# A hybrid RWKV-7 / mLSTM layer with a mixture of experts: the estimate behind TensorE's order is refitted, GpSimd's tensor work moves to VectorE and ScalarE, and the chain's PSUM tiles go into two banks

## The chip, the cores and the metric

The kernel runs on one core of one Trainium2 chip. The metric is device time in microseconds for one launch, the median of three runs. A matrix product is issued to TensorE (PE), elementwise work to VectorE (DVE), ScalarE (ACT) and GpSimd (POOL), transfers mostly from SyncE's queue (SP). In the code these engines are P, V, S, G and Y.

## The reference, cut to what matters

528 tokens (512 and 16 meta tokens) of width 1024 go through one hybrid layer and a mixture of experts, all in float32.

```
xn   = rmsnorm(h);  proj = xn @ w_in                # r, k, v | q, k, v, o, gates
# RWKV-7, 8 heads of 64, a state S of 64 x 64 per head, token by token
Sa = S @ a_t
S  = S * d_t + outer(Sa, b_t) + outer(v_t, k_t);   y_t = S @ r_t
# (low-rank products give the decay d and the gates a, g; y is normalised and gated)
# mLSTM, 4 heads, in chunks of 64 tokens, normalised and gated by sigmoid(o)
h  = h + concat(y_a, y_b) @ w_out
xn = rmsnorm(h)
# router: top-1 of 4 groups, top-2 of 8 experts in it
y[tok] += gate * ((silu(gt) * up) @ w_dn[e]),  gt, up = split(x[tok] @ w_gu[e])
```

## The kernel before, in words

**Stages.** The RWKV recurrence is turned into chunks of 64 tokens. At the start (to about 30 us) x is split into a high and a low part (`xh`, `xl`), the first two blocks of w_in are multiplied as three products of such parts, and `squares` (L613) sums x squared into the tile `acc`; two pairs of matmuls with a matrix of ones then give the norm. Up to 165 us the other blocks of w_in follow (`PLAN`, L34: one letter a block of 128 columns, each weight split into a high part by ScalarE and a low part by `lo_by` in `prepare`, L671), with four pairs of RWKV heads prepared between them (`heads`, L836, and `products`, L902). From 160 to 224 us the triangular matrices of all chunks are inverted: small blocks by VectorE elementwise (`interleaved`, L1335), the 16 meta tokens' own block by GpSimd (`inverse0`, L1357), then 32x32 matmuls (`inverse`, L1372). The chain (`chain`, L1476) runs over a chunk of 16 tokens and eight of 64, in order: `removals` and `solved` give each chunk's corrected values, `next_state` the state, `outputs` the chunk's y. To 300 us it is interleaved with what is left of the projections, of the mLSTM heads and of the states. Then come norms and gates (`outputs_a`, L1567, `gated`, L1576), the product with w_out, the router, and from 435 us the experts: 16 passes of two experts, each with 12 MB of weights.

**The order of the work.** Every instruction goes through one recording helper (line L304 of the profile). TensorE has one queue, in order. The generators of all those stages are woven into it by `Weave` (L355): by rank, and by an estimate, `Clock` (L181), of when each operand is ready. `cost` (L239) gives an instruction's duration, `slot` (L226) its place on an engine, `tell` (L273) writes end times into 16-column by 32-partition cells of each tile. A generator whose next operand the estimate puts later than now waits (`need`), and another one's matmuls are put ahead. The estimate decides the order when the program is built; on the chip each instruction waits for semaphores.

**PSUM.** `accs` has eight banks. Banks 0 to 3 are `lead`, 4 to 7 `rest`; of these 4 and 5 are `small`, 6 and 7 `wide` (L500). In the chain, `pU` takes 4 and 5 and `pY` takes 6 and 7. Each of the four banks holds one or two tiles of 256 columns: `pW` (removals) and the first half of `uv` (solved) are in 4, `pS` (next state) and the other half of `uv` in 5, the two halves of `yv` (outputs) in 6 and 7. The halves, p = 0 and p = 1, are partitions 0 to 63 and 64 to 127. ScalarE copies the first half of `uv` out and both halves of `yv`, VectorE the other half of `uv`, and VectorE adds `pS` to the decayed state `SD`, in two instructions.

```
for ch in range(-1, 8):
    removals(ch, first, vs, n);  yield from need(Wt)
    solved(ch, first, vu, n);    yield from need(vu)
    next_state(ch, first, vu, nxt)
    outputs(ch, vs, vu)
```

Of the kernel before, what the change touches and what calls it, by code (L numbers as in the profile page):

```python
# [17 lines left out]
L = 528  # L18
# [162 lines left out]
class Clock:  # L181
# [3 lines left out]
    EACH = {"V": (0.08, 1.05e-3), "S": (0.07, 0.88e-3), "G": (0.16, 0.85e-3)}  # L185
    LAG = 0.139

    def __init__(self):
        self.t = 0.0
        self.ticks = {}  # L190
        self.busy = {e: [] for e in "VSGY"}
        self.cells = {}
        self.table = None

    def cover(self, tile):

        n = int(np.prod(tile.shape[1:]))
        self.cells[tile.tensor.name] = np.zeros((2, 4, n // 16 + 1)), n

# [4 lines left out]
    def part(self, ap):  # L204
# [3 lines left out]
        c, n = self.cells[name]  # L208
# [17 lines left out]
    def slot(self, engine, ready, dur):  # L226
# [4 lines left out]
        for i, (a, b) in enumerate(busy):  # L231
            if a - ready >= dur:
                busy.insert(i, (ready, ready + dur))
                return ready
            ready = max(ready, b)
        busy.append((ready, ready + dur))
        return ready

    def cost(self, engine, op, outs, ins, kw):  # L239
# [18 lines left out]
        a, b = self.EACH[engine]  # L258
        if engine == "G" and op == "tensor_tensor":
            b = 2.1e-3  # L260
# [12 lines left out]
    def tell(self, engine, op, args, kw):  # L273
# [6 lines left out]
        ready = max(self.wrote(*ins), self.read(*outs) if engine == "P" else self.free(*outs)) + self.LAG  # L280
        if engine == "P":
            self.t = end = max(self.t, ready) + dur
        else:
            if "dma" in op:
                engine = "Y"
            end = self.slot(engine, ready, dur) + dur + (2.0 if engine == "Y" else 0)
        for ap in outs + ins:
            c = self.part(ap)
            if c is not None:
                k = 0 if any(ap is o for o in outs) else 1  # L290
                c[k] = np.maximum(c[k], end + (0.1 if engine == "P" and not k else 0))
# [19 lines left out]
class Banks:  # L311


    def __init__(self, t, clock):
        self.t, self.clock = t, clock
        clock.cover(t)
        self.busy = [False] * 8
# [118 lines left out]
def layer(ctx, tc, a, out, dbg=None, stop=None):  # L436
# [145 lines left out]
    acc = A.get([128, L], name="acc")  # L582
# [29 lines left out]
    A.put(idle_)  # L612
    def squares(k):  # L613
        sq = A.get([128, L], name="sq") if k else acc
        if k % 2:
            V.tensor_tensor(sq, xT[:, k], xT[:, k], op=OP.mult)
        else:
            S.activation(sq, xT[:, k], AF.Square)
        if k:
            G.tensor_tensor(acc, acc, sq, op=OP.add)  # L620
            A.put(sq)

    first_block(0, 2)
    for k in range(8):
# [10 lines left out]
        if k >= 2:  # L635
            proj_k(pk1, k1h, k1l, k)
            squares(k - 2)
    for k in range(6, 8):
        squares(k)

# [27 lines left out]
    def late():  # L668
        return len(every) == 8

    def prepare(kind):  # L671

        lo_by = V if late() and kind != "q" or "P3" not in W.marks else G
# [19 lines left out]
    pss = B.get(2, "pss", rest)  # L693
    for h in range(2):
        P.matmul(pss[:, h, :264], m("ones"), acc[:, 264 * h:264 * h + 264], start=True, stop=True)
# [4 lines left out]
    A.put(xT, acc)  # L700
# [135 lines left out]
    def heads():  # L836

        for j in range(4):
# [28 lines left out]
            G.tensor_scalar(r[:, NM:], r[:, NM:], c("r_k", j), 0.0, op0=OP.mult, op1=OP.add)  # L867
            G.tensor_tensor(r[:, NM:], r[:, NM:], kp[:, NM:], op=OP.mult)
# [322 lines left out]
    def states():  # L1191
# [3 lines left out]
        for tb in range(-1, 3):  # L1195
# [6 lines left out]
            kw = A.get([128, 4, 64], name="kw")  # L1202
# [154 lines left out]
    def inverse0():  # L1357
# [8 lines left out]
        yield from interleaved(G, XL0, lambda s: NL0[:, s + 1:, s], NM, tm0, 99)  # L1366
# [5 lines left out]
    def inverse():  # L1372
# [39 lines left out]
        A.put(NL, XL, Y1, Y2, *tmps, *Zs)  # L1412
        dump("X", Bt)
# [916 lines left out]
```

## Time and profile before

| what | value |
|---|---|
| median of 3 runs | 911.82 us (910.79 to 916.01) |
| profiled execution | 910.37 us |
| its span | 908.5 us |
| PE busy, share of the span | 843.5 us, 93% |
| DVE busy | 434.4 us, 48% |
| ACT busy | 270.9 us, 30% |
| POOL busy | 226.4 us, 25% |
| bytes moved by DMA | 235.56 MB, mean 259 GB/s |

The profiled execution lies 1.45 us under the median. The span runs from the first to the last record; the remaining 1.9 us are around it. Busy times of the engines overlap; the shares are means over stages that differ, and PE's 93% is made of stages in which it computes all the time and others in which it waits. A matmul of float32 is several passes, and a row's mean for one matmul is longer than what each adds to a row of many, since they are pipelined.

### The profile page before, as it was taken

The numbers are of one execution on the slowest core, as the hardware profiler recorded it, in microseconds if no ns is written. First come the engines' busy times: TensorE is split into PE (matmuls) and PEld (weight loads), VectorE is DVE, ScalarE is ACT, GpSimd is POOL, SyncE is SP. The second block draws the span as 40 slices with busy tenths as digits, with TensorE's granted clock in tenths as the row PEclk, the third lists the DMA queues.
The fourth block names the chain that finished last, engine by engine and source line by source line (L and its number), as shares of the span: only waits on it lengthen the run. The fifth ranks groups of instructions, "written<-read, shape, count | busy, mean of one in ns | idle before, by whom it ended". The sixth has DMA issues, their size and how long they took to land.

```text
span 908.5 us, 13524 instructions
## 1 busy us (share of the span) xinstructions
PE 843.5 (93%) x5385; PEld 522.1 (57%) x5386; DVE 434.4 (48%) x822; ACT 270.9 (30%) x522; POOL 226.4 (25%) x297
## 2 busy tenths in 40 slices
PE   7989889879999997998899999999999999989994
PEld 5878778769999776887334444334444333323331
DVE  7676766995544668327213334233334133322324
ACT  5666555434435773333101110011101011001102
POOL 6064544464545156254100000000000000000002
PEclk8989999987999999998899999999999999999998
DMA  7201123111100137929899999999999999999982
GB/s 237 71 3 46 47 69 83 47 47 53 51 25 25 48 107 291 403 71 335 335 402 419 420 420 420 421 420 420 420 419 421 420 421 420 420 421 421 420 341 96
DMA packets 45141, 235.56 MB, mean 259 GB/s; under 512 B 9906, under 2 KB 10290, under 8 KB 21008
## 3 DMA queue, kind: packets, MB, share of 16 engines
q1 hardware_dynamic: 42192, 228.56, 63.3%
q0 software_dynamic: 2160, 3.93, 1.2%
q10 hardware_dynamic: 720, 2.15, 0.6%
q8 instruction: 44, 0.72, 0.3%
q14 instruction: 25, 0.20, 0.1%
HBM read 234.36 MB, written 4.19 MB: 263 GB/s over the span
## 4 chain that ended last, share of the span: by engine, by line
PE 53%; DMA 24%; DVE 13%; ACT 4%; issue 2%; POOL 2%; SPq 0%; ACTq 0%; DVEq 0%; POOLq 0%
PE accs L304 25%; PE accs L2070 14%; DVE arF L304 8%; DMA arF<-wgu 7%; PE accs L2115 6%; DMA arF<-wdn 5%; DMA arM<-wgu 4%; ACT arF L304 3%; PE accs L1993 2%; DMA arH<-wgu 2%; DMA arN<-wgu 2%; DMA arN<-wdn 2%; PE accs L1994 2%; DMA arF<-wo 1%; POOL arF L304 1%
## 5 line engine op out<-in xcount | busy, mean ns | idle before, releaser
L304 PE MATMUL accs<-arS,arR 128*128 128x264 f32 (+2 forms) x1136 | 184.5, 314 | 10.2 <-DVE arR L304 5.0
L304 PEld LDWEIGHTS accs<-arS,arR 128*128 128x128 f32 (+1 forms) x1136 | 162.4, 200 | 22.5 <-DVE arR L304 5.5
L304 PE MATMUL accs<-arF 64*64 64x64 f32 (+18 forms) x1223 | 127.7, 268 | 27.5 <-DVE arF L304 17.4
L1996 DVE TENSOR_TENSOR arF<-arF,accs 128x512 f32<-128x512 f32 x124 | 80.7, 681 | 98.1 <-PE accs L1994 96.6
L304 PEld LDWEIGHTS accs<-arF 128*128 128x128 f32 (+7 forms) x1202 | 102.2, 157 | 37.3 <-DVE arF L304 11.4
L2070 PE MATMUL accs<-arF 128*64 128x512 f32 x488 | 116.4, 608 | 4.2 <-DMA arF<-wgu 4.2
L304 POOL TENSOR_TENSOR arF<-arF 128x528 f32<-128x528 f32 (+13 forms) x101 | 92.3, 917 | 67.6 <-DVE arF L304 45.4
L1804 POOL DMA_INDIRECT arM<-hd,arF x15 | 15.2, 1012 | 376.2 <-DVE arF L1794 362.7
L304 DVE TENSOR_TENSOR arF<-arF 64x16 f32<-64x16 f32 (+33 forms) x183 | 89.5, 535 | 5.1 <-POOL arF L304 2.8
L2092 ACT ACTIVATE arF<-accs,arF 128x512 f32<-128x512 f32 x16 | 11.0, 687 | 247.5 <-PE accs L2070 247.5
L2070 PEld LDWEIGHTS accs<-arF 128*64 128x64 f32 x488 | 32.6, 138 | 74.2 <-issue 57.5
L304 ACT ACTIVATE arF<-arF 128x528 f32<-128x528 f32 (+8 forms) x108 | 57.9, 559 | 49.8 <-DVE arF L304 35.5
L2125 DVE SCALAR_TENSOR_TENSOR arO<-accs,arF,arO 128x1024 fp32r<-128x1024 f32 x15 | 19.3, 1283 | 103.6 <-ACT arO L2124 103.6
L304 POOL TENSOR_SCALAR arF<-arF 64x256 f32<-64x256 f32 (+9 forms) x97 | 55.3, 572 | 42.6 <-ACT arF L304 19.6
L2115 PE MATMUL accs<-arF 128*64 128x512 f32 x280 | 62.3, 595 | 0.5 <-issue 0.5
L304 ACT COPY arF<-accs 64x256 f32<-64x256 f32 (+6 forms) x119 | 43.2, 370 | 64.1 <-PE accs L304 30.5
L1993 PE MATMUL accs<-arO,OHT 128*128 128x512 f32 x124 | 57.4, 463 | 0.0
L304 DVE TENSOR_TENSOR arF<-accs,arF 128x528 f32<-128x528 f32 (+7 forms) x81 | 35.4, 460 | 34.1 <-PE accs L304 20.6
L1994 PE MATMUL accs<-arO,OHT 128*128 128x512 f32 x124 | 48.9, 394 | 0.0
L2070 PE MATMUL accs<-arN,arF 128*64 128x512 f32 x200 | 47.1, 599 | 1.6 <-DMA arN<-wgu 1.6
L304 PE MATMUL accs<-arW,arS 128*128 128x512 f32 x192 | 47.8, 406 | 0.0
L2070 PE MATMUL accs<-arM,arF 128*64 128x512 f32 x200 | 46.7, 599 | 1.0 <-DMA arM<-wgu 0.9
(141 smaller groups left out, 932.6 us busy)
## 6 DMA issues: line engine op xcount, KB each, us to landing
arF<-wgu SPq DMA_DIRECT2D x61, 1024.0 KB, 19.8
arF<-wdn SPq DMA_DIRECT2D x35, 1024.0 KB, 20.1
arN<-wgu SPq DMA_DIRECT2D x25, 1024.0 KB, 19.9
arM<-wgu SPq DMA_DIRECT2D x25, 1024.0 KB, 19.8
arH<-wgu SPq DMA_DIRECT2D x16, 1024.0 KB, 19.9
arN<-wdn SPq DMA_DIRECT2D x15, 1024.0 KB, 19.9
arF<-wb SPq DMA_DIRECT2D x23, 512.0 KB, 3.6
arH<-wdn SPq DMA_DIRECT2D x5, 1024.0 KB, 19.8
```

Source lines behind the costliest of these rows:

```text
L304: r = f(*args, **kw)
L1804: nc.gpsimd.indirect_dma_start(out=xt[p % 2], out_offset=None, in_=hd, in_offset=bass.IndirectOffsetOnAxis(ap=idx[:, p % 2:p % 2 + 1], axi ...
L1993: P.matmul(pq, lhs, oh[:, hs], start=True, stop=False)
L1994: P.matmul(pq, lhs, ol[:, hs], start=False, stop=True)
L1996: V.tensor_tensor(hv, hv, pq, op=OP.add)
L2070: P.matmul(pgu[64 * e:64 * e + 64, h], x[:, k, 64 * e:64 * e + 64], w[:, D * e + 512 * h:D * e + 512 * h + 512], start=(k == 0), stop=(k = ...
L2092: S.activation(av, pgu[:, 0], AF.Silu, scale=r1_)
L2115: P.matmul(pdn[64 * e:64 * e + 64, h], aT[:, k, 64 * e:64 * e + 64], w[:, D * h + 512 * e:D * h + 512 * e + 512], start=(k == 0), stop=(k ...
L2125: V.scalar_tensor_tensor(ol, pdf, g1_, oh.bitcast(F32), op0=OP.mult, op1=OP.subtract)
```

## The change

In the estimate: new constants for ScalarE, GpSimd, matmuls by shape and the scan; a shorter delay (`NEAR`, 0.07) between instructions of one engine; an engine `X` that stands for the port which GpSimd and a VectorE instruction with two wide inputs in SBUF share, so that the estimate puts them one after the other. In the work: the squares go to ScalarE and their pairwise sums to VectorE, with four pairs of ones-matmuls in place of one pair, and no sum on GpSimd; three tensor products a head and the product with r_k go from GpSimd to VectorE; two copies into E a head go from GpSimd to ScalarE; `inverse0` and the gate of `gated` go to VectorE; the low parts of weights that are made between the products of the last pair of heads and the end of the inverse go from GpSimd to VectorE. In the chain: `uv` and `pW` lie in one bank, `pS` and `yv` in the other, and the two banks of `pY` are free for others. Some tiles of the end are taken in other places (`Gw`, `kw`, `sq`, `yT`).

```diff
-    EACH = {"V": (0.08, 1.05e-3), "S": (0.07, 0.88e-3), "G": (0.16, 0.85e-3)}
-    LAG = 0.139
+    EACH = {"V": (0.08, 1.05e-3), "S": (0.13, 0.88e-3), "G": (0.17, 0.9e-3)}
+    LAG, NEAR = 0.139, 0.07
...
-            m = size(ins[0])
-            n, passes = size(ins[1]), 2 if op == "transpose" else 4
+            m, n = size(ins[0]), size(ins[1])
             if ins[1].dtype == F32R and n >= 256 or ins[1].dtype == BF16:
-                passes = 1
-            dur = max(n, m) * passes / 2400 * (0.7 if m <= 64 and passes > 1 else 1.0)
+                passes, dur = 1, max(n * 1.09 / 2400, 0.056)
+            elif op == "transpose":
+                passes, dur = 1, 0.11
+            else:
+                passes, dur = 4, 2 * max(n * 2.05 / 2400, 0.055 if m <= 64 else 0.11)
...
+            if engine == "G" or engine == "V" and len(wide_) > 1:
+                engine += "X"
             end = self.slot(engine, ready, dur) + dur + (2.0 if engine == "Y" else 0)
...
     def squares(k):
-        sq = A.get([128, L], name="sq") if k else acc
+        sqs2.append(A.get([128, L], name="sq"))
+        S.activation(sqs2[k], xT[:, k], AF.Square)
         if k % 2:
-            V.tensor_tensor(sq, xT[:, k], xT[:, k], op=OP.mult)
-        else:
-            S.activation(sq, xT[:, k], AF.Square)
-        if k:
-            G.tensor_tensor(acc, acc, sq, op=OP.add)
-            A.put(sq)
+            V.tensor_tensor(sqs2[k], sqs2[k], sqs2[k - 1], op=OP.add)
...
-        lo_by = V if late() and kind != "q" or "P3" not in W.marks else G
+        lo_by = V if late() and kind != "q" or "inverse" not in W.marks else G
...
-            G.tensor_tensor(MV[:, :, 128:192], i64[:, None].to_broadcast([128, 8, 64]),
+            V.tensor_tensor(MV[:, :, 128:192], i64[:, None].to_broadcast([128, 8, 64]),
...
-            G.tensor_tensor(nk, nk, al, op=OP.mult)
+            V.tensor_tensor(nk, nk, al, op=OP.mult)
...
-            G.tensor_tensor(kp, kp, kx[j], op=OP.mult)
+            V.tensor_tensor(kp, kp, kx[j], op=OP.mult)
...
-                    (S.copy if p else gcopy)(E[i][PAR[p], :, j, p], MV[PAR[p], 4 * i:4 * i + 4, 0:128])
+                    S.copy(E[i][PAR[p], :, j, p], MV[PAR[p], 4 * i:4 * i + 4, 0:128])
...
-        yield from interleaved(G, XL0, lambda s: NL0[:, s + 1:, s], NM, tm0, 99)
+        yield from interleaved(V, XL0, lambda s: NL0[:, s + 1:, s], NM, tm0, 99)
...
-                P.matmul(uv[o, p, j], (X0[PAR[p], j] if first else Bt[PAR[p], ch, j, 0:64]), Wt[PAR[p], j],
+                P.matmul(uv[o, j], (X0[PAR[p], j] if first else Bt[PAR[p], ch, j, 0:64]), Wt[PAR[p], j],
...
-        pY = yield from bank(2, "pY", wide)
-        pW, pS = (pU[:, i, 256:512].rearrange("p (j x) -> p j x", j=4) for i in range(2))
-        uv = pU[:, :, 0:256].rearrange("p a (j x) -> p a j x", j=4)
-        yv = pY[:, :, 0:256].rearrange("p a (j x) -> p a j x", j=4)
+        (uv, pW), (pS, yv) = ([pU[:, i, 256 * h:256 * h + 256].rearrange("p (j x) -> p j x", j=4) for h in range(2)]
+                              for i in range(2))
...
-        G.tensor_tensor(y, y, Gw[:, :, 128 * tb:128 * tb + 128], op=OP.mult)
+        V.tensor_tensor(y, y, Gw[:, :, 128 * tb:128 * tb + 128], op=OP.mult)
```

What this moves shows in the instruction order at three places. The first is TensorE's queue in one chunk of the chain, with the semaphores that an instruction waits for in brackets. Before, eight matmuls of `next_state` (the first two rows) are followed by the sixteen of `outputs` (`arE` is the tile E), then by two matmuls of a projection:

```order
596 L304 MATMUL accs<-arF 64x64 [waits DVE_49,Activation_49]
597 L304 MATMUL accs<-arF 64x64 x7
598 L304 MATMUL accs<-arE_255,arF 64x64 x8
599 L304 MATMUL accs<-arF 64x64 x8
600 L304 MATMUL accs<-arS_68,arR 128x264 x2
```

With the change the same matmuls stand in the same order, followed by the next chunk's `removals`:

```order
623 L336 MATMUL accs<-arF 64x64 x4
624 L336 MATMUL accs<-arF 64x64 [waits DVE_49]
625 L336 MATMUL accs<-arF 64x64 x3
626 L336 MATMUL accs<-arE_258,arF 64x64 [waits DVE_49]
627 L336 MATMUL accs<-arE_258,arF 64x64 x7
628 L336 MATMUL accs<-arF 64x64 x4
629 L336 MATMUL accs<-arF 64x64 [waits Activation_49]
630 L336 MATMUL accs<-arF 64x64 x3
631 L336 MATMUL accs<-arF,arE_258 64x64 x8
```

The wait for ScalarE ahead of `next_state` is gone from this place, and two waits are new: `outputs` waits for VectorE before its first matmul, and for ScalarE before the second half's own four.

The second is the same queue at `solved`, a few rows earlier. Before, its eight matmuls stand behind one wait, between projections:

```order
587 L304 MATMUL accs<-arS_68,arR 128x264 [waits Pool_49]
588 L304 MATMUL accs<-arS_68,arR 128x264
589 L304 MATMUL accs<-arF 64x64 [waits DVE_49]
590 L304 MATMUL accs<-arF 64x64 x7
591 L304 MATMUL accs<-arS_68,arR 128x264 x2
```

and with the change:

```order
608 L336 MATMUL accs<-arS_68,arR 128x264 x2
609 L336 MATMUL accs<-arF 64x64 [waits DVE_49]
610 L336 MATMUL accs<-arF 64x64 x3
611 L336 MATMUL accs<-arF 64x64 [waits Activation_49]
612 L336 MATMUL accs<-arF 64x64 x3
613 L336 MATMUL accs<-arS_68,arR 128x264 x2
```

The second half now waits for ScalarE, which copies the first half out of the bank.

The third is GpSimd's queue while VectorE inverts. Before, the small steps of `inverse0` alternate with the low parts of weights (128x1024):

```order
92 L304 TENSOR_TENSOR arR<-arF,arR 128x1024
93 L304 TENSOR_TENSOR arF<-arF 128x63
94 L304 TENSOR_TENSOR arF<-arF 128x7x9
95 L304 TENSOR_TENSOR arF<-arF 128x64
96 L304 TENSOR_TENSOR arF<-arF 128x8x8
97 L304 TENSOR_TENSOR arF<-arF 128x63
```

With the change the queue holds at that place:

```order
49 L336 TENSOR_TENSOR arF<-arF 128x512 x2
50 L336 TENSOR_SCALAR arF<-arF 64x4x64 x2
51 L336 TENSOR_SCALAR arF<-arF 128x64
52 L336 MEMSET arF 128x3 x2
53 L336 TENSOR_SCALAR arF<-arF 64x4x64 x2
54 L336 MEMSET arF 128x256
55 L336 TENSOR_TENSOR arF<-arF 128x528
```

Those steps and the low parts have left GpSimd; they stand in VectorE's queue.

## Rows read from the trace of the kernel before

**Rows 1.** Busy times by stretch: us, engines (instructions), PEclk, DMA share, GB/s

```profile
195.00:298.00 103.00, 103.00 (x1311) 95.69 (x1310) 56.21 (x120) 45.16 (x87) 52.89 (x74) 0.89 0.11 34
410.00:435.00 25.00, 18.94 (x187) 17.31 (x186) 20.40 (x80) 7.62 (x26) 9.72 (x13) 0.81 0.91 340
...
656.00:860.00 204.00, 196.65 (x970) 73.80 (x966) 63.50 (x114) 20.82 (x28) 5.95 (x6) 1.00 1.01 420
```

**Rows 2.** The chain that ended last, around 655 us: start, us, what

```profile
654.60 1.44 PE accs L2070 x7
656.04 20.48 DMA arM<-wgu
```

**Rows 3.** Waits of PE, 0 to 435 us: in total, times, longest

```profile
PE accs L304 <- DVE arF L304: 18.4, 10, 6.0
PE accs L304 <- ACT arF L304: 8.1, 12, 2.0
...
PE accs L304 <- DVE arS L304: 3.1, 3, 2.0
```

**Rows 4.** Timeline of the start (PE, then DVE, then POOL): start, us, instructions, idle before

```profile
10.52 5.68 PE L304 MATMUL accs<-arS,arR 128*128 128x264 f32 x25 [2.00 <-DVE arS L304]
25.72 1.05 PE L304 MATMUL accs<-arF 128*128 128x264 f32 x4
27.93 0.75 PE L304 MATMUL accs<-arS,arQ 128*128 128x264 f32 x4 [1.16 <-ACT arQ L304]
17.44 0.79 DVE L304 SCALAR_TENSOR_TENSOR arS<-arF,arS 128x528 fp32r<-128x528 f32 x1
19.90 4.44 DVE L304 SCALAR_TENSOR_TENSOR arS<-arF,arS 128x528 fp32r<-128x528 f32 x3
17.76 6.02 POOL L304 TENSOR_TENSOR arF<-arF 128x528 f32<-128x528 f32 x4
```

**Rows 5.** Timeline, first pair of heads: DVE, POOL, PE

```profile
60.90 3.64 DVE L304 TENSOR_TENSOR arF<-arF 64x512 f32<-64x512 f32 x1 [2.84 <-POOL arF L304]
62.69 2.99 POOL L304 TENSOR_TENSOR arF<-arF 128x528 f32<-128x528 f32 x2
66.66 3.83 PE L304 MATMUL accs<-arF 128*128 128x192 f32 x12 [3.29 <-POOL arF L304]
```

**Rows 6.** Timeline of the elementwise inverse: DVE, POOL twice, PE

```profile
173.88 17.66 DVE L304 TENSOR_TENSOR arF<-arF 128x96 f32<-128x96 f32 x44
179.13 2.48 POOL L304 TENSOR_TENSOR arR<-arF,arR 128x1024 fp32r<-128x1024 f32 x1 [0.21 <-ACT arR L304]
181.57 4.62 POOL L304 TENSOR_TENSOR arF<-arF 128x63 f32<-128x63 f32 x10
194.25 2.62 PE L304 MATMUL accs<-arF 128*128 128x128 f32 x10 [6.00 <-DVE arF L304]
```

**Rows 7.** Timeline, norms and gates: DVE, PE

```profile
349.34 1.21 DVE L304 TENSOR_TENSOR arR<-arF,arR 128x1024 fp32r<-128x1024 f32 x1
350.61 5.64 PE L304 MATMUL accs<-arS,arR 128*128 128x512 f32 x17 [5.03 <-DVE arR L304]
```

**Rows 8.** Busy times of three shorter stretches, columns as in rows 1

```profile
9.00:15.80 6.80, 5.28 (x24) 5.28 (x25) 6.80 (x6) 5.85 (x10) 5.12 (x4) 0.50 1.05 382
193.30:200.10 6.80, 5.86 (x25) 5.22 (x26) 6.73 (x21) 1.87 (x6) 5.27 (x10) 0.50 0.01 2
213.80:227.40 13.60, 13.60 (x222) 13.29 (x221) 5.98 (x8) 5.14 (x10) 2.64 (x5) 0.50 0.20 66
```

**Rows 9.** Timeline of one chunk of the chain: PE, then DVE, then ACT

```profile
260.32 0.64 PE L304 MATMUL accs<-arE,arF 128*64 128x64 f32 x13
260.89 0.96 PE L304 MATMUL accs<-arF 64*64 64x64 f32 x16
261.78 0.69 PE L304 MATMUL accs<-arF,arE 128*64 128x64 f32 x16
260.60 0.88 DVE L304 TENSOR_TENSOR arF<-accs,arF 64x256 f32<-64x256 f32 x2 [2.19 <-PE accs L304]
261.60 0.75 ACT L304 COPY arF<-accs 64x256 f32<-64x256 f32 x2 [0.66 <-PE accs L304]
```

More of the change, by code (lines that the diff above doesn't have):

```diff
@@ L190, in __init__ @@
         self.ticks = {}
-        self.busy = {e: [] for e in "VSGY"}
-        self.cells = {}
+        self.busy = {e: [] for e in "VSGYX"}
+        self.cells, self.who = {}, {}
         self.table = None
@@ L207, in part @@
             return None
-        c, n = self.cells[name]
+        c, n = (self.who if who else self.cells)[name], self.cells[name][1]
+        c = c if who else c[0]
         per = 2 if ap.dtype == BF16 else 1
@@ L232, in slot @@
             if a - ready >= dur:
-                busy.insert(i, (ready, ready + dur))
-                return ready
+                return i, ready
             ready = max(ready, b)
-        busy.append((ready, ready + dur))
-        return ready
+        return len(busy), ready
+    def slot(self, engines, ready, dur):
+        while True:
+            at = [self.gap(e, ready, dur) for e in engines]
+            last = max(t for _, t in at)
+            if all(t == last for _, t in at):
+                break
+            ready = last
+        for e, (i, t) in zip(engines, at):
+            self.busy[e].insert(i, (t, t + dur))
+        return last
     def cost(self, engine, op, outs, ins, kw):
@@ L279, in tell, with known @@
         dur = self.cost(engine, op, outs, ins, dict(kw, rest=args))
-        ready = max(self.wrote(*ins), self.read(*outs) if engine == "P" else self.free(*outs)) + self.LAG
+        me = 1 + "PVSG".find(engine) if "dma" not in op else 9
+        def known(aps, k):
+            t = 0.0
+            for ap in aps:
+                c = self.part(ap)
+                if c is not None:
+                    t = max(t, float((c[k] + np.where(self.part(ap, True)[k] == me, self.NEAR, self.LAG)).max()))
+            return t
+        ready = max(known(ins, 0), known(outs, 1), 0.0 if engine == "P" else known(outs, 0))
         if engine == "P":
@@ L285, in tell @@
                 engine = "Y"
+            wide_ = [x for x in ins if int(np.prod([k for _, k in list(x.ap)[1:]])) > 1 and x.tensor.name != self.accs]
+            if engine == "G" or engine == "V" and len(wide_) > 1:
+                engine += "X"
             end = self.slot(engine, ready, dur) + dur + (2.0 if engine == "Y" else 0)
@@ L290, in tell @@
                 k = 0 if any(ap is o for o in outs) else 1
-                c[k] = np.maximum(c[k], end + (0.1 if engine == "P" and not k else 0))
+                new = end + (0.1 if me == 1 and not k else 0)
+                self.part(ap, True)[k][c[k] <= new] = me
+                c[k] = np.maximum(c[k], new)
 class Told:
@@ L316, in __init__ @@
         clock.cover(t)
+        clock.accs = t.tensor.name
         self.busy = [False] * 8
@@ L612, in layer, with summed @@
     A.put(idle_)
+    pss = B.get(2, "pss", rest)
+    sqs2 = []
     def squares(k):
-        sq = A.get([128, L], name="sq") if k else acc
+        sqs2.append(A.get([128, L], name="sq"))
+        S.activation(sqs2[k], xT[:, k], AF.Square)
         if k % 2:
-            V.tensor_tensor(sq, xT[:, k], xT[:, k], op=OP.mult)
-        else:
-            S.activation(sq, xT[:, k], AF.Square)
-        if k:
-            G.tensor_tensor(acc, acc, sq, op=OP.add)
-            A.put(sq)
+            V.tensor_tensor(sqs2[k], sqs2[k], sqs2[k - 1], op=OP.add)
+    def summed(k):
+        for h in range(2):
+            P.matmul(pss[:, h, :264], m("ones"), sqs2[k][:, 264 * h:264 * h + 264], start=(k == 1), stop=(k == 7))
     first_block(0, 2)
@@ L636, in layer @@
             proj_k(pk1, k1h, k1l, k)
-            squares(k - 2)
-    for k in range(6, 8):
         squares(k)
+        if k == 5:
+            summed(1)
+        if k == 7:
+            summed(3)
     W = Weave(clock, B)
@@ L692, in layer @@
     A.put(*kput, *kput1)
-    pss = B.get(2, "pss", rest)
-    for h in range(2):
-        P.matmul(pss[:, h, :264], m("ones"), acc[:, 264 * h:264 * h + 264], start=True, stop=True)
+    summed(5)
+    summed(7)
     rstd = A.get([128, L], name="rstd")
@@ L699, in layer @@
     B.put(pss)
-    A.put(xT, acc)
+    A.put(xT, *sqs2)
     dump("rstd", rstd)
@@ L1201, in states @@
                 P.transpose(pk[:n, 128 * b:128 * b + 128], qk[2 + b][:, tk], ident)
-            kw = A.get([128, 4, 64], name="kw")
+            kw, = yield from W.room(A, 1, [128, 4, 64], F32, "kw")
             V.scalar_tensor_tensor(kw[:n], pk[:n, 0:256].rearrange("p (h x) -> p h x", h=4), 1.0 / 16,
@@ L1412, in inverse @@
         A.put(NL, XL, Y1, Y2, *tmps, *Zs)
+        W.mark("inverse")
         dump("X", Bt)
@@ L1515, in chain @@
                 W.mark(f"yT{ch // 2}")
-        A.put(Vs, *VS, *VU, Wt, SD, DT)
-        Gw = A.get([128, 4, T], name="Gw")
-        sqs.append(A.get([128, 4, 4, 128], name="sq"))
-        B.put(pU, pY)
-        every.extend(rest)
+        A.put(*VS, *VU, Wt, SD, DT)
+        B.put(pU)
+        Gw, = yield from W.room(A, 1, [128, 4, T], F32, "Gw")
+        sqs.extend((yield from W.room(A, 4, [128, 4, 128], F32, "sq")))
+        every.extend(small)
         W.mark("chain")
```

37 lines of the change are left out of this document (20 added, 17 removed).

## The prediction, as it was put on record

> **What bounds the kernel now.** I read from the end backwards. The chain that ended last shows at 656 us the point where TensorE stops setting the pace: until there it runs through matmuls, from there through transfers of expert weights of some 20 us each [rows 2]. From 656 to 860 us the DMA engines are full (1.00, 420 GB/s, [rows 1]), and TensorE has a little room. The bytes are the same after the change, and their transfers start when buffers come free in the stages before 435 us, so the end follows the start: if everything before 435 us ends X earlier, the expert part starts and ends about X earlier. So I look for X in the first 435 us, and there the busy times by stretch and the waits of TensorE say where it stands. From 195 to 298 us, in the chain, it is busy for 103.00 of 103.00 us [rows 1]: whatever is added there is paid in full. In 410 to 435 us it idles for 6.1 us [rows 1], in the router, which the change doesn't touch. The rest of its idle time is spread over waits for VectorE (18.4 us), ScalarE (8.1) and the first low parts of x (3.1) [rows 3], one wait of 3.3 for GpSimd [rows 5] and one of 5.03 for the low part of a weight [rows 7].
>
> Why is VectorE late? The timelines show that its instructions with two inputs in SBUF get slow while GpSimd runs a tensor product. At the start three that take 0.79 us alone take 4.44 together while GpSimd adds four squares in 6.02 [rows 4]; a product of 64x512, no more elements a partition than those, takes 3.64 us while GpSimd works [rows 5]; in the inverse each small step waits for GpSimd's small steps and for weight parts of 2.48 us [rows 6].
>
> **The change, part by part.** The sum is made against the profiled execution, 910.37 us; the median is 1.45 higher.
>
> *Start.* GpSimd's additions go, ScalarE takes all squares, VectorE has as many instructions as before but without the delay: three of them at 0.79 instead of 4.44 together give 2.1 us. On TensorE the waits of 3.1 us [rows 3] and 1.16 [rows 4] should go. Three more pairs of ones-matmuls at 1.05 us [rows 4] cost 3.15. The clock stood at 0.50 (1.2 GHz) from 9.0 to 15.8 us, around the wait of 2.00 [rows 4, 8]; with the wait gone, I give half of the 2.6 us that these matmuls (5.28 us busy) would save at 2.4 GHz, 1.3. Net: 3.1 + 1.16 - 3.15 + 1.3 = **+2.4** (0 to 5).
>
> *Heads and inverse, 30 to 210 us.* The waits for VectorE are 18.4 us [rows 3]; without the router's 6.1 they are 12.3, of which 6.00 stand behind the inverse [rows 6]. VectorE takes over work (three products and one more a pair of heads, some 30 small steps, about six low parts of 1.21 us [rows 7]), but loses its stalls, and the two are about equal; a late result that was late through a stall comes early, one that was late through work doesn't. I take three quarters: 9.2. The wait for GpSimd, 3.3 [rows 5], goes. Of ScalarE's 8.1 [rows 3] I take a third, 2.7, since it gets two copies a pair of heads more. Together **+15.2** (5 to 20). GpSimd's queue gets shorter; what waits for it there gains, too, and no price is put on that.
>
> *Norms and gates.* The low part at 349.34 us stood behind the work of `gated`, stalled by GpSimd, and TensorE waited for 5.03 us [rows 7]. With the gate on VectorE and the low part earlier, 0.7 are left: **+4.3** (3 to 5).
>
> *Clock after waits.* Six stretches of 3.4 to 6.8 us between 53 and 354 us, 27.3 us in all, run at 0.50 behind such waits; the one at 193.3 us is shown [rows 8]. Were all at full clock, 13.6 us would come back. I take somewhat over a third: **+5** (0 to 13).
>
> *Order.* The refitted estimate puts the 32x32 matmuls of the inverse about 84 projection matmuls later, and leaves 126 instead of 234 for the chain. Work only changes places, on an engine that has no holes there: 0. But it is the cover for waits in the chain, and that matters next.
>
> *The chain in two banks.* The order of the instructions shows three new waits a chunk. `solved`'s second half waits until ScalarE has copied the first half out of the same bank; `outputs` waits until VectorE has read `pS`, which now lies in `yv`'s bank, with both additions; and its second half waits for ScalarE again. Nothing stands behind them that TensorE could do: its queue is in order, and the estimate, which looks at cells of 16 columns, not at banks, has put no other work there. In the chunk at 260 us the additions begin at 260.60 and end at 261.48, while the matmuls of `outputs` ran from 260.32 without waiting [rows 9]: with the wait these would begin 1.2 us later. ScalarE's copies take 0.37 each (0.75 for two) and the first begins at 261.60, 0.23 after the first half of the row of 0.96 [rows 9]; with a little until the matmul starts this is 0.63 each. So 7 times 1.2 (the chain's last chunk has no next state) are 8.4; 8 times 0.63 in `outputs` and 9 times in `solved` are 10.7. ScalarE is busy for 45.16 and VectorE for 56.21 of those 103 us [rows 1], so now and then a copy stands behind something else; 2 us for that. Sum **-21** (-15 where some are short, -26). Bounds for the whole term from both sides: 0, if the results were always there already; and all at half clock, which is a rival.
>
> A rule speaks about these waits. The Trainium skill, "PSUM — Partial Sum Buffer", section "PSUM bank collisions raise a hardware error", says that two engines must be kept apart by bank and quadrant of 32 partitions, and that different quadrants of one bank may be accessed together. By it the halves p = 0 and p = 1, on partitions 0 to 63 and 64 to 127, need not wait for each other: the 10.7 us would be 0 and the time about 895 us. The order, however, shows the waits in the program, halves or not, and the sum goes by that; no trace here shows yet what each costs.
>
> Sum: 2.4 + 15.2 + 4.3 + 5 - 21 = 5.9 us. 910.37 - 5.9 = 904.5, and with 1.45 on top, **906 us**. The change takes away about 27 us of waits and puts 21 into the stage that had none.
>
> **Rivals.**
>
> *Slower: the chain loses its clock.* Small matmuls do not hold it: from 213.8 to 227.4 us TensorE was busy all the time with 222 of them, and the granted clock was 0.50 [rows 8]. In the chain the projections between the chunks held it up. Now about half of these are gone from there, and each chunk has 2.5 us of waits. If the chain's own matmuls, 0.96 + 0.69 + 0.64 and as much as the first again for `solved` and `next_state`, some 3.9 us a chunk and 35 for nine, run at 1.2 GHz half of the time, that costs 17 us: 906 + 17 = 923. It decides from a mean clock under about 0.8 in the chain. Against it: the planner still puts 12 to 24 projection matmuls next to each step until the sixth chunk. Chance 0.17.
>
> *Faster: the waits cost little.* They stand where the copy is done when TensorE comes, because VectorE and ScalarE are quicker without GpSimd, or because the halves' waits come to nothing as in the rule above. With 10.7 of the 21 gone it is 895, with all gone 885; I take 890. For it: GpSimd's stalls also delay the chain's additions. Against it: the copy can't start before its own matmuls end, so 0.37 and the way there and back are always there. Chance 0.20.
>
> *No change: VectorE becomes what TensorE waits for.* It takes over all of GpSimd's work in the inverse and the low parts there. If half of the 15.2 us is not recovered, the sum is -1.7: 913 or so. For it: VectorE is already the engine that is waited for most [rows 3]. Against it: a good part of its time now is stalls, as in the 3.64 us [rows 5]. Chance 0.15.
>
> *The stages before don't matter*, since transfers set the end. Against it: the transfers wait for buffers that the stages before set free, so the stream can't start earlier by itself, nor stay behind. 912 us; chance 0.03.
>
> **How the numbers follow.** A measurement of this kernel can tell about 0.5%, 4.6 us, from no change: faster is below 907.3, slower above 916.4. My forecast has 0.45; its terms' bounds spread it to about 896 to 917, so just over half of it is faster, some 0.25, most of the rest the same, 0.17, and 0.03 slower. The waits that cost little give 0.20 faster. The clock gives 0.17 slower. VectorE as the bound gives 0.02 faster, 0.10 the same and 0.03 slower, the transfers 0.03 the same. Together: faster 0.47, same 0.30, slower 0.23. The range from 889 to 921 takes in the forecast's whole spread, half of the faster rival and part of the slow one.
>
> **What would show it.** In the profile after: TensorE's waits in the chain, for ScalarE some 17 times 0.6 us and for VectorE 7 times 1.2, where there were none; no long VectorE instruction beside GpSimd in the first 50 us; the low part of 349 us no longer 5.03 us late; the elementwise inverse shorter and the wait of 6.00 mostly gone; the router's 6.1 us as before; and the stretch of full DMA as long as before, earlier by X. I am wrong if the chain shows no new idle time (then 890), if its clock falls below 0.8 (then 923), or if the waits before 210 us have only moved to other places.

## The result, and the profile after

The change takes 959.9 us (median of 4 runs, 955.26 to 963.36) against 911.88: ratio 1.0515, interval 1.0459 to 1.0571, some 47 us slower. The profiled execution, the slowest of the four, took 963.36 us with a span of 961.1. The busy times by stretch show where the time stands; columns as in [rows 1]. First the change, from 0 to 30 us, 75 to 125 us and in the chain (here from the first to the last matmul that uses E):

```profile
0.00:30.00 30.00, 27.24 (x169) 23.36 (x171) 19.47 (x35) 22.18 (x32) 4.48 (x13) 0.94 0.64 215
75.00:100.00 25.00, 20.62 (x102) 18.56 (x102) 15.14 (x26) 13.82 (x24) 6.38 (x13) 0.80 0.07 22
100.00:125.00 25.00, 23.34 (x154) 22.07 (x155) 13.02 (x23) 14.46 (x27) 4.38 (x5) 0.86 0.11 43
242.40:346.80 104.40, 85.72 (x817) 74.48 (x817) 31.94 (x65) 29.36 (x67) 23.90 (x45) 0.70 0.04 13
700.00:900.00 200.00, 191.66 (x938) 70.19 (x934) 59.17 (x106) 19.49 (x26) 5.95 (x6) 1.00 1.01 420
```

The same stretches of the kernel before:

```profile
0.00:30.00 30.00, 22.54 (x117) 17.83 (x119) 23.58 (x31) 14.51 (x22) 16.77 (x20) 0.88 0.60 197
75.00:100.00 25.00, 22.74 (x160) 20.46 (x158) 18.65 (x28) 15.32 (x28) 10.04 (x15) 1.00 0.16 43
100.00:125.00 25.00, 21.08 (x147) 19.09 (x148) 18.45 (x28) 14.56 (x28) 11.35 (x18) 1.00 0.13 43
236.68:299.99 63.31, 63.31 (x860) 58.05 (x859) 33.36 (x63) 29.17 (x61) 31.30 (x46) 0.97 0.08 25
```

The reader is to see three things. The start is better: 169 matmuls instead of 117 by 30 us, 12 of the 52 being the additional ones-matmuls. Between 75 and 100 us that lead is lost, with 102 matmuls against 160, and up to 125 us the clock is at 0.80 and 0.86 where it was 1.00, though the idle time of both rows together is the same (6.0 us after, 6.2 before). And the chain has grown from 63.31 to 104.40 us: with nearly as many matmuls it has 18.7 us of idle time where there was none, and its clock is at 0.70 instead of 0.97. The transfers at the end run as before (1.01, 420 GB/s), only later.

In one chunk at 271 us, where the clock is still nearly full, the new waits stand one by one. TensorE, then VectorE and ScalarE:

```profile
270.97 0.68 PE L336 MATMUL accs<-arF 64*64 64x64 f32 x8
272.10 0.68 PE L336 MATMUL accs<-arF 64*64 64x64 f32 x8 [0.46 <-ACT arF L336]
...
274.31 0.97 PE L336 MATMUL accs<-arF 128*64 128x64 f32 x16
276.31 0.69 PE L336 MATMUL accs<-arE,arF 128*64 128x64 f32 x16 [1.04 <-DVE arF L336]
276.92 0.68 PE L336 MATMUL accs<-arF 64*64 64x64 f32 x8
278.10 0.68 PE L336 MATMUL accs<-arF 64*64 64x64 f32 x8 [0.50 <-ACT arF L336]
```

```profile
275.38 0.88 DVE L336 TENSOR_TENSOR arF<-accs,arF 64x256 f32<-64x256 f32 x2 [1.25 <-PE accs L336]
```

```profile
271.68 0.37 ACT L336 COPY arF<-accs 64x256 f32<-64x256 f32 x1 [0.60 <-PE accs L336]
277.68 0.37 ACT L336 COPY arF<-accs 64x256 f32<-64x256 f32 x1 [5.64 <-PE accs L336]
```

Each wait ends with the reader of the shared bank: the second half of `solved` with ScalarE's copy of the first, `outputs` with VectorE's additions, its second half with ScalarE again. In [rows 9] `next_state`, `outputs` and the next `removals` followed each other with no idle time. A step that is cut in two is also busy for longer: sixteen matmuls take 0.97 us in one (the row at 274.31), eight and eight 0.68 each. The waits of TensorE as a list, first from 0 to 470 us, then in the chain alone:

```profile
PE accs L336 <- ACT arF L336: 31.6, 27, 4.0
PE accs L336 <- DVE arF L336: 16.9, 18, 2.2
```

```profile
PE accs L336 <- ACT arF L336: 11.1, 15, 2.7
PE accs L336 <- DVE arF L336: 7.6, 7, 1.6
```

ScalarE's share has grown from 8.1 us in 12 waits [rows 3] to 31.6 in 27, but only 11.1 of these, in 15 waits, stand in the chain. The waits of 3.3 us for GpSimd [rows 5], of 6.00 behind the inverse [rows 6] and of 5.03 for a low part [rows 7] are gone; new ones stand ahead of the chain and behind it, the longest 4.04 us.

### The profile page after: what moved, and what is told of

It reads as the page before. It is cut to its first block, busy times and chain, and to the rows that moved or that the text cites. A ratio compares the mean times of both kernels' runs of the same rounds, so it can differ in the third digit from the quotient of the medians.

```text
span 961.1 us, 13535 instructions
## 1 busy us (share of the span) xinstructions
PE 878.3 (91%) x5397; PEld 551.8 (57%) x5398; DVE 434.5 (45%) x879; ACT 286.1 (30%) x541; POOL 150.2 (16%) x221
## 5 line engine op out<-in xcount | busy, mean ns | idle before, releaser
L336 PE MATMUL accs<-arF 32*32 32x32 f32 (+17 forms) x1235 | 156.1, 298 | 37.5 <-ACT arF L336 28.4
L336 PE MATMUL accs<-arS,arR 128*128 128x264 f32 (+2 forms) x1152 | 188.0, 317 | 2.0 <-ACT arS L336 1.0
L336 PEld LDWEIGHTS accs<-arS,arR 128*128 128x128 f32 (+1 forms) x1152 | 167.0, 203 | 14.5 <-issue 4.8
L336 PEld LDWEIGHTS accs<-arF 128*128 128x128 f32 (+8 forms) x1214 | 124.9, 180 | 56.1 <-ACT arF L336 31.4
L336 DVE TENSOR_TENSOR arF<-arF 128x512 f32<-128x512 f32 (+32 forms) x229 | 83.1, 416 | 1.1
L336 ACT ACTIVATE arF<-arF 128x528 f32<-128x528 f32 (+6 forms) x115 | 61.5, 553 | 58.6 <-DVE arF L336 37.3
L336 POOL TENSOR_SCALAR arF<-arF 64x256 f32<-64x256 f32 (+9 forms) x93 | 52.4, 566 | 147.6 <-PE accs L336 51.6
L1842 POOL DMA_INDIRECT arM<-hd,arF x15 | 15.2, 1012 | 373.1 <-DVE arF L1832 359.5
L336 POOL TENSOR_TENSOR arF<-arF 64x256 f32<-64x256 f32 (+7 forms) x44 | 40.7, 928 | 111.4 <-DVE arF L336 101.5
L336 DVE TENSOR_TENSOR arF<-accs,arF 128x128 f32<-128x128 f32 (+7 forms) x81 | 35.2, 460 | 32.2 <-PE accs L336 19.7
L336 DVE SCALAR_TENSOR_TENSOR arF<-arF 128x528 f32<-128x528 f32 (+5 forms) x55 | 39.4, 719 | 20.4 <-ACT arF L336 18.6
```

Source lines behind the costliest of these rows:

```text
L336: r = f(*args, **kw)
L1842: nc.gpsimd.indirect_dma_start(out=xt[p % 2], out_offset=None, in_=hd, in_offset=bass.IndirectOffsetOnAxis(ap=idx[:, p % 2:p % 2 + 1], axi ...
```

## The experiments

Each run is compared with runs of the kernel before on the same chip. Four tiles of the end (`Gw`, `kw`, `sq`, `yT`) are taken in other places by the change, and the kernel with two banks doesn't fit without that. So the steps from one kernel to the other are: the places, the moved work, the estimate, the two banks.

### Which part costs the time

**The change with four banks.** `uv`, `pW`, `pS` and `yv` as before, all else from the change.

```diff
-        (uv, pW), (pS, yv) = ([pU[:, i, 256 * h:256 * h + 256]...
+        pY = yield from bank(2, "pY", wide)
+        pW, pS = (pU[:, i, 256:512]...
+        uv = pU[:, :, 0:256]...
+        yv = pY[:, :, 0:256]...
```

> The change with the chain in four banks again (uv, pW, pS and yv as before, two tiles of uv and yv), all else kept: the estimate, the moved work, the tiles' places. Theory A (the shared banks): the new waits, and the clock that the waits cost, are the whole loss; without them the chain is dense again, its clock above 0.9, and the time is 895 to 912 us. Theory B (the fill): the projections that have gone from between the chain's chunks (270 matmuls before, 168 with the change, 174 here) are what held the clock; the chain stays at 0.6 to 0.8, only the waits' own 21 us and a part of the clock come back, and the time is 925 to 945 us.

916.77 us, ratio 1.0044 (1.0018 to 1.0071), some 5 us above theory A's range and 8 below theory B's. The chain is 66.68 us long and its clock 0.90, with nearly the same projections in it:

```profile
237.78:304.46 66.68, 62.55 (x815) 55.42 (x815) 33.22 (x66) 30.83 (x69) 26.06 (x47) 0.90 0.05 17
```

The two banks cost 43 us. In the profiled executions 37.7 of the difference stand in the chain; it also starts 4.6 us later with two banks, and some 6 come behind it, and where these two come from isn't settled. Theory B falls: with 144 projection matmuls in this stretch the chain is nearly dense, with 216 before. (This counts from the first matmul that uses E. The expectations count from the chain's first matmul, some 10 us earlier, and come to 30 to 54 more.)

**Two banks alone**, without the moved work and with the old estimate (the chain's lines of the diff of the change, on the kernel before, and the places).

> The kernel before with the chain in two banks (and the places of some tiles of the end taken as in the change, without which it does not fit), the old estimate, no work moved. 252 projection matmuls stand in the chain. Theory A: the waits stand here too, 20 to 25 us in the chain, and with them the clock falls: 930 to 960 us. Theory B: the waits cost their 21 us, the clock holds since the fill is there: 925 to 935 us, with the chain's clock above 0.9.

946.54 us, ratio 1.0381 (1.0341 to 1.0422). Against its base, the places alone (below), 29 us. The chain takes 94.81 us at 0.89:

```profile
237.99:332.80 94.81, 76.99 (x849) 66.29 (x849) 36.23 (x67) 35.91 (x77) 30.36 (x49) 0.89 0.08 26
```

So with 198 projection matmuls in the chain the same waits cost 29 us, with 138 they cost 43, at a clock of 0.89 against 0.70. That more fill is what holds the clock better isn't shown: the two kernels differ in the moved work, too.

**The moved work alone**, four banks, the old estimate, the places.

> The kernel before with GpSimd's work moved as in the change (squares, heads, the small inverse, the gate, the low parts), the places of some tiles as in the change, the old estimate and four banks. 156 projection matmuls stand in the chain. Theory A: no shared banks, so the chain keeps its clock: 895 to 912 us. Theory B: the fill is gone from the chain, its clock falls to 0.7 or so: 925 to 945 us.

913.73 us, ratio 1.0027 (1.0002 to 1.0053), 2 us above theory A's range: hardly a loss, so theory A again, and no gain either. With some 100 projection matmuls its chain is shorter than before, at a clock of 0.97:

```profile
243.99:302.88 58.89, 55.47 (x822) 48.86 (x821) 32.66 (x70) 28.55 (x64) 24.77 (x45) 0.97 0.04 11
```

**The change with the old estimate.**

> The change with the old estimate (constants, costs by shape and no shared port), all else as in the change; 162 projection matmuls stand in the chain, 168 with the new one. Both theories put the loss in the chain and none in the estimate: 945 to 965 us. If the refitted estimate were itself the cause, this would be near 930 us or under it.

960.29 us, ratio 1.053 (1.0482 to 1.0578): with two banks the estimate makes no difference. The chain has some 108 projection matmuls here, and the clock is at 0.70 as with 138:

```profile
246.62:349.10 102.48, 84.16 (x827) 71.26 (x827) 32.95 (x70) 29.95 (x66) 25.82 (x46) 0.70 0.05 17
```

### Wait by wait

From the change with four banks, one kind of wait at a time: both halves of `uv` in one bank; the first half of `yv` beside `pS`; both halves of `yv` in one bank. In each, everything else has a bank as before.

```diff
-        uv = pU[:, :, 0:256].rearrange("p a (j x) -> p a j x", j=4)
+        uv = pU[:, 0, 0:256].rearrange("p (j x) -> p j x", j=4)
```

> The change with four banks, but both halves of uv in one: only the nine waits in solved are there (each by the rows of before some 0.63 us, 5.7 in all). The change with four banks took 916.8 us. If waits and the clock they cost add up wait by wait (43 us for 24 waits of 21 us together: each microsecond waited costs two), this is about 928 us; if single waits cost only themselves and the clock falls when all three kinds are there, about 922 us.

> The change with four banks, but the first half of yv beside pS: only the seven waits of outputs for VectorE's additions are there (some 1.2 us each, 8.4 in all). Wait by wait with its clock: about 934 us; waits alone: about 925 us.

> The change with four banks, but both halves of yv in one: only the eight waits of outputs' second half for ScalarE are there (0.63 us each, 5.0 in all). Wait by wait with its clock: about 927 us; waits alone: about 922 us.

They took 921.08 us (ratio 1.0099, 1.0063 to 1.0135), 933.61 (1.0250, 1.0201 to 1.0298) and 924.98 (1.0142, 1.0103 to 1.0182). Over the ratio 1.0044 of four banks these are 5.0, 18.8 and 8.9 us, each known to 4 or 5 us by the intervals, for 5.7, 8.4 and 5.0 us of waits as priced in the prediction; together 32.7 us, and all at once 43. The chains of the three, in the same order:

```profile
242.71:319.74 77.03, 69.66 (x815) 61.49 (x815) 31.93 (x66) 30.52 (x68) 24.16 (x45) 0.84 0.04 14
242.65:322.16 79.51, 66.03 (x815) 57.91 (x815) 32.78 (x66) 31.04 (x69) 24.26 (x45) 0.87 0.04 14
239.77:314.75 74.98, 67.72 (x816) 59.62 (x815) 33.05 (x66) 30.85 (x69) 24.85 (x45) 0.86 0.04 15
```

By the times, the first kind costs itself, the second more than twice its price, and the third lies between the two forecasts. The traces don't bear out that division. With each kind alone the clock falls from 0.90 to between 0.84 and 0.87, and TensorE's busy time in the chain grows by 7.1, 3.5 and 5.2 us, most in the first (whose profiled execution was the slowest of six). And of the 18.8 us of the second the chain holds 12.8; where the rest comes from isn't settled. What is shown is that each kind costs time and clock by itself; how the 43 us divide among them is not.

**The waits filled.** The change, with 62 bf16 matmuls put ahead of the new waits, into a bank that is never read; they compute nothing that is used.

```diff
+    def cover(n):
+        one = m("ones").bitcast(BF16)[:, 0:128]
+        for _ in range(n):
+            P.matmul(pD, one, one[:, None].to_broadcast([128, 4, 128]), start=True, stop=True)
```

> The change as it is, with bf16 matmuls of 128x512 put ahead of each new wait, into a bank that nobody reads: two ahead of the second half of solved and of outputs, four ahead of the first half of outputs, 62 in all, 13 us at full clock, which fits inside the waits. If a good part of the loss is the clock that falls in the chain (the windows of the change show 0.50 to 0.84 from 235 to 355 us, some 30 us), these matmuls hold it up and the time falls from 960 to 930 to 942 us, with the chain's clock above 0.9. If the waits alone are the loss, it stays at 955 to 965 us.

948.25 us, ratio 1.0389 (1.0344 to 1.0434), between the two forecasts. The chain:

```profile
242.32:331.51 89.19, 86.64 (x865) 64.66 (x865) 31.28 (x65) 30.51 (x68) 24.34 (x45) 0.87 0.04 14
```

Useless work in the waits makes the kernel 12 us faster, since the clock in the chain rises from 0.70 to 0.87. The waits themselves are as long as they were, only filled: `solved` at 275.52 us takes 1.85 us with its two useless matmuls, and 1.81 in the chunk at 271 us above with its wait. So the chains give an estimate of what is wait and what is clock. With four banks the chain takes 66.68 us, here 89.19 at nearly the same clock, and with the change 104.40: some 22.5 us for the waits themselves and 15.2 for the clock.

### Where the forecast gain went

**The places alone**, and **no low parts in the inverse** (the change with four banks; six low parts are left out and zeros take their place), then the moved work **without the inverse** and **in the inverse alone**.

> The kernel before with nothing but the places of the end's tiles (Gw, kw, sq, yT) taken as in the change: the base of the runs with two banks alone and with the moved work alone. Both theories: no difference, 909 to 914 us.

> The change with four banks, but the six low parts of weights made during VectorE's inverse are left out (ScalarE writes zeros in their place, so these blocks are multiplied with their high parts and zeros). VectorE has 7.4 us less to do there, TensorE as much as before. Theory C (VectorE's inverse, and not TensorE's idle time before it, sets when the chain can start): the 32x32 matmuls start 6 to 8 us earlier than 211 us, and the end comes 4 to 8 us earlier than with four banks alone, 907 to 912 us. Rival (TensorE's work sets it): within 2 us of four banks alone, 914 to 917 us.

> The kernel before with the moved work except in the inverse: squares, heads and gate as in the change; the small inverse and its low parts stay on GpSimd; old estimate, four banks. Theory C: the start is some 4 us ahead, but the elementwise inverse starts at 160 us or later all the same and takes 48 us; 907 to 913 us, no difference to the kernel before. Rival (waits removed ahead of the inverse are a gain): 10 us of waits gone, 899 to 904 us.

> The kernel before with only the inverse's work moved (small inverse and low parts to VectorE); old estimate, four banks. In the order 84 projection matmuls are left in the chain, before 198 to 216. Theory C: the elementwise inverse takes 46 to 48 us as before, and the chain has less to cover its waits with: 912 to 920 us. Rival (GpSimd's stalls were the loss in the inverse): 902 to 907 us.

The places took 917.24 us (1.0067, 1.0050 to 1.0085): expected was no difference, and they cost 4.6 to 7.7 us. Without the low parts 908.65 (0.9966, 0.9952 to 0.9981), 7 to 8 us less than with them. Without the inverse 922.38 (1.0120, 1.0096 to 1.0145), above both forecasts and slower than its base, the places, by 5; the inverse alone 913.97 (1.0047, 1.0021 to 1.0072). The second and fourth times lie in theory C's ranges, but its mechanism is not what the traces show. It has the 32x32 matmuls, and with them the chain, start when VectorE's inverse is done. The elementwise inverse runs between VectorE's transposes. In the change it goes from 162.97 to 212.5 us, without the low parts from 162.60 to 206.0:

```profile
162.97 1.25 DVE L336 STREAM_TRANSPOSE arF<-arF 128x1024 f32<-128x1024 f32 x1 [1.62 <-ACT arF L336]
...
210.39 2.08 DVE L336 STREAM_TRANSPOSE arF<-arF 128x1024 f32<-128x1024 f32 x1
```

```profile
162.60 1.25 DVE L336 STREAM_TRANSPOSE arF<-arF 128x1024 f32<-128x1024 f32 x1 [1.60 <-ACT arF L336]
...
202.80 3.19 DVE L336 STREAM_TRANSPOSE arF<-arF 128x1024 f32<-128x1024 f32 x2
```

In the kernel before it starts and ends at much the same times, 160.54 and 211.3:

```profile
160.54 1.25 DVE L304 STREAM_TRANSPOSE arF<-arF 128x1024 f32<-128x1024 f32 x1 [1.86 <-POOL arF L304]
...
208.12 3.19 DVE L304 STREAM_TRANSPOSE arF<-arF 128x1024 f32<-128x1024 f32 x2
```

VectorE's stalls in this stretch are gone, and the low parts it took over fill the same time:

```profile
L336 DVE TENSOR_TENSOR arR<-arF,arR 128x1024 fp32r<-128x1024 f32 x6 | 7.4, 1235 | 0.0
```

But TensorE doesn't idle just ahead of the 32x32 matmuls. Until they start it runs through projections that the estimate has put there, in the kernel before [rows 1] as in the others. Without the low parts the inverse is done at 206.0 us, and the 32x32 matmuls start at 209.37, behind 36 projection matmuls where there are 96 in the change and with four banks (the edit changes the order, too):

```profile
204.82 4.62 PE L336 MATMUL accs<-arS,arR 128*128 128x264 f32 x36
209.37 13.25 PE L336 MATMUL accs<-arF 32*32 32x32 f32 x256
```

With four banks they start at 211.27, so 1.9 us have been gained there and not the 6 to 8 expected. Most of the rest stands among these matmuls. In the change they fall into two halves with a wait between them (TensorE, ScalarE, VectorE, GpSimd):

```profile
223.41 6.83 PE L336 MATMUL accs<-arF 32*32 32x32 f32 x128 [4.04 <-ACT arF L336]
222.11 0.64 ACT L336 ACTIVATE arF<-arF 128x528 f32<-128x528 f32 x1 [3.95 <-DVE arF L336]
217.73 4.29 DVE L336 SCALAR_TENSOR_TENSOR arF<-arF 128x528 f32<-128x528 f32 x1
222.79 0.71 DVE L336 SCALAR_TENSOR_TENSOR arF<-arF 128x528 f32<-128x528 f32 x1
218.04 2.33 POOL L336 TENSOR_TENSOR arR<-arF,arR 128x1024 fp32r<-128x1024 f32 x1
```

TensorE waits for ScalarE's copy, ScalarE for VectorE, and VectorE's instruction takes 4.29 us beside GpSimd's tensor products, where another of the same form takes 0.71 at 222.79. With four banks the wait is 4.07 us. It is absent without the low parts, in the kernel before, and with the moved work under the old estimate, which has 12 projection matmuls at this place. So a stall of VectorE by GpSimd, of the kind that the change was to remove, has come up in a new place.

**What the places cost.** ScalarE's timeline in the run with the places alone shows table loads between logarithms (`accs,arF`) and exponentials; `sq` is one tile with one exponential before, four with four after:

```profile
312.38 1.28 ACT L304 ACT_TABLE_LOAD   x1
314.65 0.69 ACT L304 ACTIVATE arF<-accs,arF 128x512 f32<-128x512 f32 x1 [0.99 <-PE accs L304]
315.36 1.28 ACT L304 ACT_TABLE_LOAD   x1
316.65 0.63 ACT L304 ACTIVATE arF<-arF 128x512 f32<-128x512 f32 x1
317.30 1.28 ACT L304 ACT_TABLE_LOAD   x1
```

From 250 to 430 us ScalarE loads tables 4 times in the kernel before and 8 times here, 10.3 us; the change has 8, too. Four runs keep the exponentials behind all logarithms, by a zero that VectorE takes from all four tiles:

```diff
+        z = A.get([128, 1], name="z")
+        V.tensor_scalar(z, sqs[0][:, 0, 0:1], 0.0, 0.0, op0=OP.mult, op1=OP.add)
+        for sq in sqs[1:]:
+            V.scalar_tensor_tensor(z, sq[:, 0, 0:1], 0.0, z, op0=OP.mult, op1=OP.add)
         for sq in sqs:
-            S.activation(sq, sq, AF.Exp, scale=-0.5)
+            S.activation(sq, sq, AF.Exp, scale=-0.5, bias=z)
```

> The run with the tiles' places alone (917.2 us), with the four exponentials behind all four logarithms (a value of zero taken from all four tiles is added in each). Theory D (the places cost their table loads): two of four extra loads are gone, 912 to 915 us. Rival (the places cost something else, such as a wait for room): 916 to 918 us.

> The run with the moved work alone (913.7 us), with the exponentials behind all logarithms; no extra table load is left. Theory D: 907 to 910 us, which would be faster than the kernel before by the 3.5 us that the moved work gave over its base. Rival: 912 to 915 us.

> The change with four banks (916.8 us), with the exponentials behind all logarithms. Theory D: 910 to 913 us. Rival: 915 to 918 us.

> The run with the inverse's work alone moved (914.0 us), with the exponentials behind all logarithms. Theory D: 907 to 911 us. Rival: 912 to 915 us.

With the whole moved work it is 904.00 us, ratio 0.9919 (0.9894 to 0.9945), the fastest kernel here; with the refitted estimate, too, 908.33 (0.9964, 0.9942 to 0.9986). Both lie below theory D's ranges: the loads cost more than their own time. The run with four banks shows how. Two waits of TensorE and one of VectorE, for results that stand in ScalarE's queue between the loads:

```profile
318.73 3.26 PE L336 MATMUL accs<-arF 64*128 64x129 f32 x16 [4.10 <-ACT arF L336]
327.83 1.13 PE L336 MATMUL accs<-arF 128*64 128x129 f32 x8 [5.83 <-DVE arF L336]
325.94 0.16 DVE L336 SCALAR_TENSOR_TENSOR arF<-arF 128x4 f32<-128x4 f32 x1 [10.22 <-ACT arF L336]
```

With the exponentials behind, 0.79 us are left of TensorE's two:

```profile
323.79 0.66 PE L336 MATMUL accs<-arF 128*64 128x129 f32 x8 [0.79 <-DVE arF L336]
```

The places alone stay at 919.52 (1.0096, 1.0062 to 1.0129) and the inverse alone at 916.55 (1.0054, 1.0028 to 1.0080), above both forecasts, though their loads are down from 8 to 6 and to 4: there the theory fails, and what the places cost in those two isn't settled. The refitted estimate, which makes no difference with two banks, costs some 4 us with four (908.33 against 904.00, just clear of the noise); the wait of 4 us among the 32x32 matmuls is in the first of these two runs (3.98) and not in the second.

## Why the prediction was wrong

The prediction of 906 us failed on both sides of its sum: of the gains of 27 us nearly nothing arrived at the end, and the term of -21 us was 43.

- **The chain's waits, -21.** The mechanism was right, and the waits stand where the order showed them: 22 in the chain, with 18.7 us of idle time. Most of those for ScalarE idle 0.46 to 0.50 us, and with the 0.39 that a step cut in two is busy longer they cost some 0.9 each, where 0.63 was priced. By the run with filled waits all of them cost some 22.5 us themselves, which is the term's size. The step that failed is that the sum put what the waits do to the chain's clock at nothing and left it to a rival: it fell to 0.70, which by the same run cost some 15.2 us more, and 0.50 was granted from 290 to 330 us, behind the two longest waits (1.55 and 2.69 us). The rest of the 43 us stands outside the chain. The rival "the chain loses its clock" was this, with the point from which it decides. Its chance of 0.17 was too low; its price of 17 us is near the 15.2, and its 923 us failed mainly because it was set on top of gains that weren't there. (Its 3.9 us a chunk don't come out of its terms, which give 3.25 or 4.21, with the first once or twice more; the price is then 15 or 19.) The evidence was at hand [rows 8]: a busy stretch at half clock, nearly without fill. The words against it, that projections stand next to each step until the sixth chunk, took fill next to a wait for fill in it.
- **The Trainium skill's rule.** By the Trainium skill, "PSUM — Partial Sum Buffer", section "PSUM bank collisions raise a hardware error", different quadrants of one bank may be accessed together, so that the halves need not wait for each other. This program waits by bank all the same, in the trace mostly 0.46 to 0.50 us each time. The two kinds of waits between halves cost 5.0 and 8.9 us alone. No run here has the halves in one bank without that wait. The Trainium skill, "Perfetto Trace Analysis", section "Matmuls", asks for independent groups of matmuls to go round different banks, so that one is read out while the next computes. By the run with four banks that is worth 43 us here.
- **Start, +2.4.** Right: the waits of 2.00 and 1.16 us are gone and the matmuls by 30 us are 52 more, 12 of them ones-matmuls.
- **Heads and inverse, +15.2.** The step that failed is that the waits for VectorE, GpSimd and ScalarE are gains once their causes are moved. From 30 us to the 32x32 matmuls, TensorE's idle time has gone from 23.0 to 19.1 us, before and after:

```profile
30.00:210.90 180.90, 157.87 (x1067) 147.28 (x1065) 137.77 (x254) 97.90 (x185) 88.56 (x137) 0.93 0.17 49
30.00:212.62 182.62, 163.51 (x1111) 153.11 (x1110) 136.99 (x303) 102.65 (x196) 40.78 (x76) 0.93 0.17 52
```

  The wait of 6.00 us behind the inverse is gone, but up to 160 us there is more idle time than before, 14.8 us instead of 12.6. So the waits before 210 us have in good part only moved, which was one of the signs of being wrong. What was gained is work done early: 972 projection matmuls instead of 888 come ahead of the 32x32 ones, which start at 212.62 us instead of 210.90. Of that the new wait of 4.04 us among them takes back a part. The early projections were also the cover of the chain, which with four banks has 4.1 us of idle time where there was none. The step "Order: 0" failed with it, also in its cause: the moved work alone, under the old estimate, has the same 972. That VectorE becomes what is waited for was the rival of 0.15; it is so at the wait of 4.04 us, through a stall beside GpSimd and not through the work taken over.
- **Norms and gates, +4.3.** The wait of 5.03 us [rows 7] is gone, but others stand nearby, 1.42 us for ScalarE and 1.91 for VectorE:

```profile
390.38 0.49 PE L336 MATMUL accs<-arW 128*128 128x512 f32 x1 [1.42 <-ACT arW L336]
392.79 2.74 PE L336 MATMUL accs<-arW 128*128 128x512 f32 x7 [1.91 <-DVE arW L336]
```

  With four banks these two come to 0.2 us, but the 4.10 and 5.83 us between the table loads stand there instead.
- **Clock after waits, +5.** Nothing came: from 30 us to the 32x32 matmuls the mean clock is 0.93 before and after (the two rows above). From 75 to 125 us it is lower, 0.80 and 0.86 where it was 1.00. New waits of 1.65, 2.18, 1.13 and 1.32 us stand there, but as the idle time is the same in sum, that they are the reason isn't shown.
- **The end follows the start** was right: the last matmul with w_out comes 56 us later in the profiled executions, the end 53. (The 1.00 that the prediction reads as the DMA engines' share in [rows 1] is TensorE's clock; their share is 1.01.)

## What to carry to other kernels

A wait in a dense stretch costs itself and what the clock gives up for it: here 43 us for waits priced at 21, and 12 came back with useless matmuls in them. Before tiles are put into one bank, look in the instruction order for a new wait between one half's reader and the other half's writer, and ask what stands in the queue to fill it. Idle time that goes is not yet a gain: ask what the work that is now done early was covering later, and where two engines that were kept apart will now meet.

## What was not expected of the hardware

Splitting one tile into four changed ScalarE's order so that logarithms and exponentials alternate, each change with a table load of 1.28 us; keeping them apart was worth 9.7 us in the best kernel, more than the four loads' 5.1 us, and nothing in two others. And 62 matmuls whose results nobody reads made a kernel faster by 1.2%.
